# Four reorderings in a one-core encoder step: scaling by the final norm, a deferred pair, the root's argument, a later total

## The chip, the cores and the metric

The kernel runs on one core of a Trainium2 chip. The core has five engines that run side by side and wait for each other by semaphores: TensorE (PE in the profile, with its weight loads as PEld), VectorE (DVE), ScalarE (ACT), GpSimd (POOL) and SyncE (SP). Transfers between device memory and on-chip memory are issued by SP, ACT or POOL. The metric is the time of one execution on the device in microseconds (us); the median of several runs counts.

## The reference

One layer of a streaming encoder on 576 rows (512 of a prompt and 64 of a running stream) with 1024 features, in float32:

```python
x = x + 0.5 * swiglu_ffn(rms_norm(x, ffn1_norm), ffn1_w_gate_up, ffn1_w_down)
h = rms_norm(x, mix_norm); p = h @ w_in
a_b, a_c, a_v, b_u, gate_a, gate_b = jnp.split(p, cuts, axis=-1)
a_conv, new_a = causal_depthwise_conv(a_c * a_v, hist_a, conv_a_w)       # 3 taps
y_a = (a_b * a_conv) @ w_a_out
glu = b_u[..., :D_B] * jax.nn.sigmoid(b_u[..., D_B:])
b_conv, new_b = causal_depthwise_conv(glu, hist_b, conv_b_w)             # 31 taps
y_b = jax.nn.silu(layer_norm(b_conv + conv_b_bias, ...)) @ w_b_out
x = x + (jax.nn.sigmoid(gate_a) * y_a + jax.nn.sigmoid(gate_b) * y_b) @ w_out
x = x + 0.5 * swiglu_ffn(rms_norm(x, ffn2_norm), ffn2_w_gate_up, ffn2_w_down)
y = rms_norm(x, final_norm)                                              # 0.5 is the macaron half step
```

`swiglu_ffn` is `(silu(gate) * up) @ w_down` with 2816 hidden features; `rms_norm` divides by the root of the mean of squares.

## The kernel before

Features lie on the 128 partitions and rows along the free axis: X is eight tiles of 128 x 576 (`X[0]` to `X[7]`). Every product is made in float32 accuracy from three products of rounded parts: a weight and an activation are each split into a high part (`fp32r`) and the low rest, and `mm` issues high x high, high x low and low x high, for two halves of 288 rows. So a product of one output tile over 1024 inputs is 8 x 6 = 48 matmuls, and its result lies in one of four PSUM buffers (tag `mm`, two banks each).

**Weights.** `Stream` keeps them coming. SP loads a raw block (`raw`, six buffers); ACT rounds it into the high part (CAST) and writes its negative into the low part's buffer (ACTIVATE); POOL issues a transfer that adds the raw block to that (`DMA_DIRECT2D u<-raw`, `g<-raw` or `act<-raw`). So a unit's low part is there when that transfer has landed. `get(n)` starts the units up to six ahead. In the two feed-forward stages a hidden tile is made from seven half-sized products instead of eight (`pair`; a scheme after Strassen), for which sums of raw blocks are made on DVE (`w<-raw,raw`, `w<-w,raw`), and whose low parts come from a DVE subtraction (`g<-w,g`, `u<-w,u`).

**Order.** Nothing reorders the instructions: each engine runs them as the code issues them. `product` issues the matmuls of one tile, and what follows them on DVE and ACT is kept back (`behind`) until the next product's matmuls are issued; `rest` is the same for steps of `pair`, of which one is taken up after each of the next pair's seven products.

**Norms.** `Sum` adds up the squares of the eight tiles; `gather` splits the sum and `total` multiplies it by ones on PE, which adds over the partitions. `rstd` makes the reciprocal root of a total: ACT's Abs_reciprocal_sqrt reads the total, DVE's `tensor_scalar` makes the argument `a` from it, and three DVE steps refine the root to `R`. ACT functions sit in tables; a function of another table brings an `ACT_TABLE_LOAD` into ACT's stream. `table(func)` calls a function on one column so that its table is loaded there.

**The stages.** First feed-forward `f1` (from 28 us in the profile), with plain pairs for the first three hidden tiles; `finish1` with the last group's products and the squares of the new X; the mixer with its two convolutions (DVE's taps); LayerNorm in steps that `advance` takes up between the products `("p", 5, j)` and `("ya", j)`: stage 1 subtracts the mean, stage 2 gathers the squares, stage 3 makes the root `RL`; then the second branch, the output projection `("o", j)` in the order `IN_TURN`, and the second feed-forward `f2` with one plain pair (`PLAIN = {"f1": 3, "f2": 1}`). Its last group (`finish2`) makes the tiles 2 to 7 (`LATE`) in two spans of rows (`LATE_SPANS`, 304 and 272 rows), so that the output of the first span leaves while the second is computed; `put` scales the eight tiles by the final norm (ACT), makes the root, multiplies (POOL for the first span, DVE and POOL for the second) and issues the output's transfers.

Of the kernel before, what the change touches and what calls it, by code (L numbers as in the profile page):

```python
# [11 lines left out]
ALU = mybir.AluOpType  # L12
# [91 lines left out]
def tile_encoder_step(  # L104
# [435 lines left out]
    def rstd(total, spans=HALVES):  # L540
# [135 lines left out]
    def ffn(f, xg, sums, finish, forms, R=None, todo=()):  # L676
# [5 lines left out]
        def plain(i, hs):  # L682
# [92 lines left out]
    def finish1(g, hs):  # L775
        ps = both([("f1", "d", g, j) for j in range(2)], hs)
# [199 lines left out]
    stage = [0]  # L976

    def advance():
# [58 lines left out]
    forms = Forms(R_N2)  # L1037
    for n, j in enumerate(IN_TURN):
# [18 lines left out]
    def finish2(g, hs):  # L1057
# [10 lines left out]
        def put(spans, engines, pieces, queues):  # L1068

            i, e = spans[0]  # L1070
            n = e - i
            ys = []
            for q in range(KT // 2):
                yt = gtile(n=2 * n).rearrange("p (a n) -> p a n", a=2)
                for a in range(2):
                    sca.activation(
                        yt[:, a, :], X[2 * q + a][:, i:e], AF.Copy, scale=par(2 * q + a, R_NF)
                    )
                ys.append(yt)
            RF = rstd(fsum, spans)[:, i:e]  # L1080
            for n, (q, a, size) in enumerate(pieces):
                for b in range(a, a + size):
                    engines[q].tensor_tensor(ys[q][:, b, :], ys[q][:, b, :], RF, op=ALU.mult)
                queues[n % 2].dma_start(ydst[q, :, a : a + size, i:e], ys[q][:, a : a + size, :])

        for spans in LATE_SPANS:
            i, e = spans[0]
            fsum.n = LATE[0]
            for j in LATE:
                if i == 0:  # L1090
# [4 lines left out]
                xj = X[j][:, i:e]  # L1095
# [3 lines left out]
                if i > 0 and j == LATE[0]:  # L1099
                    put(  # L1100
# [60 lines left out]
```

## Time and profile before

| | |
|---|---|
| median of 3 runs | 1324.33 us (1319.91, 1324.33, 1324.44) |
| the profiled execution | 1321.72 us, of which 1319.9 from the first to the last instruction (the span) |
| mean granted TensorE clock | 0.994 |
| DVE, ACT, POOL busy | 895.2, 776.6, 400.9 us |
| transfers | 217.22 MB, 165 GB/s in the mean |
| table loads on ACT | 10, of 1.28 us |

Times are from the start of the span. A row of a timeline has the start, the length, the engine, the source line (a helper's line, 80, for nearly all), the operation, out<-in by tile names, the sizes, how many equal instructions are merged, and in brackets the engine's idle time before it with what ended it. A row of windows has the stretch, its length, the busy time (and count) of PE, PEld, DVE, ACT and POOL, then the granted clock, the transfers' share and GB/s.

### The profile page before, as it was taken

The page shows a single profiled execution, that of the slowest core. Times are in us where ns is not written, and L with a number is a line of the kernel's source. Part 1 is how long each engine was busy: PE and PEld are TensorE (multiplying, and loading weights), DVE is VectorE, ACT ScalarE, POOL GpSimd, SP SyncE. Part 2 cuts the span into 40 slices and gives each one's busy share as a digit, 9 for nine tenths or more (in the row PEclk, how much of TensorE's full clock was granted, in tenths as well). Part 3 has the DMA queues.
Part 4 walks back from the last instruction along what each step waited for, and adds up shares of the span by engine and source line. Part 5 has one row for each costly group of instructions (what it writes and reads, how often), then busy time and mean ns, then how long its engine had stood idle before and what let it go on. Part 6 is the DMA issues. An engine that isn't in the chain of part 4 may idle for free.

```text
span 1319.9 us, 25704 instructions
## 1 busy us (share of the span) xinstructions
PE 1292.0 (98%) x9746; PEld 1286.4 (97%) x9746; DVE 895.2 (68%) x1468; ACT 776.6 (59%) x1369; POOL 400.9 (30%) x504
## 2 busy tenths in 40 slices
PE   8999999999999999999999999999899999999995
PEld 8999999999999999999999999999899999999995
DVE  6848758748845999889884061337757858847944
ACT  8655656646766655555545574466665655645663
POOL 4142332332243454322322322221242242231242
PEclk9999999999999999999999999999999999999997
DMA  9497787886798898777875977775687797796692
GB/s 244 103 183 160 157 181 159 173 187 143 154 198 175 172 205 178 168 168 170 173 162 120 201 161 154 167 150 129 133 177 162 154 193 156 158 210 139 152 181 76
DMA packets 289564, 217.22 MB, mean 165 GB/s; under 512 B 15648, under 2 KB 251168, under 8 KB 289440
## 3 DMA queue, kind: packets, MB, share of 16 engines
q0 software_dynamic: 60192, 99.12, 45.7%
q1 hardware_dynamic: 227504, 115.62, 30.8%
q8 instruction: 77, 1.26, 0.4%
q10 hardware_dynamic: 1744, 0.84, 0.2%
q14 instruction: 47, 0.39, 0.1%
HBM read 113.81 MB, written 2.62 MB: 88 GB/s over the span
## 4 chain that ended last, share of the span: by engine, by line
PE 71%; issue 12%; DMA 6%; DVE 4%; ACT 4%; POOL 2%; POOLq 0%; DVEq 0%; SPq 0%; ACTq 0%
PE mm L80 71%; DMA u<-raw 2%; DVE tmp L80 1%; DMA raw<-in_ffn_w_gate_up_dram 1%; DMA raw<-in_ffn_w_down_dram 1%; DMA g<-raw 1%; ACT g L80 1%; ACT tmp L80 1%; ACT act L80 1%; ACT u L80 1%; POOL g L80 1%; DVE acc L80 1%; DVE w L80 1%; DVE g L80 1%; DMA act<-raw 1%
## 5 line engine op out<-in xcount | busy, mean ns | idle before, releaser
L80 PE MATMUL mm<-act,u 128*128 128x288 f32 x4668 | 661.1, 294 | 1.7 <-DMA u<-raw 1.5
L80 PEld LDWEIGHTS mm<-act,u 128*128 128x128 f32 x4668 | 630.9, 188 | 2.4 <-DMA u<-raw 2.1
L80 PE MATMUL mm<-act,g 128*128 128x288 f32 x2748 | 396.4, 294 | 6.1 <-DMA g<-raw 3.8
L80 PEld LDWEIGHTS mm<-act,g 128*128 128x128 f32 x2748 | 374.0, 188 | 7.5 <-DMA g<-raw 4.7
L80 POOL DMA_DIRECT2D u<-raw x203 | 177.0, 872 | 553.1 <-ACT u L80 497.0
L80 PE MATMUL mm<-act,act 128*128 128x288 f32 (+2 forms) x2280 | 314.0, 294 | 2.6 <-DVE act L80 1.6
L80 PEld LDWEIGHTS mm<-act,act 128*128 128x128 f32 x2280 | 303.7, 188 | 4.0 <-DVE act L80 2.3
L80 POOL DMA_DIRECT2D g<-raw x123 | 107.3, 873 | 256.7 <-ACT g L80 202.4
L80 DVE SCALAR_TENSOR_TENSOR w<-g,prm,w 128x606 f32<-128x606 f32 x232 | 179.2, 842 | 1.4 <-ACT w L80 1.4
L80 ACT CAST u<-raw 128x512 fp32r<-128x512 f32 (+2 forms) x203 | 116.4, 574 | 100.6 <-PE mm L80 81.7
L80 DVE TENSOR_TENSOR tmp<-mm,tmp 128x288 f32<-128x288 f32 (+1 forms) x244 | 109.5, 457 | 73.4 <-PE mm L80 56.1
L80 ACT ACTIVATE u<-u 128x512 fp32r<-128x512 f32 (+2 forms) x203 | 120.6, 594 | 6.4
L80 POOL DMA_DIRECT2D act<-raw x92 | 80.9, 879 | 55.5 <-ACT act L80 54.6
L80 ACT CAST g<-raw 128x512 fp32r<-128x512 f32 (+2 forms) x123 | 67.2, 547 | 42.4 <-PE mm L80 15.6
L80 DVE SCALAR_TENSOR_TENSOR tmp<-mm,r 128x576 f32<-128x576 f32 x48 | 36.3, 757 | 78.4 <-PE mm L80 78.4
L80 ACT CAST act<-tmp 128x576 fp32r<-128x576 f32 x84 | 56.3, 674 | 55.6 <-DVE tmp L80 54.7
L80 ACT CAST g<-w 128x512 fp32r<-128x512 f32 x80 | 49.5, 619 | 65.3 <-DVE w L80 59.0
L80 ACT CAST u<-w 128x512 fp32r<-128x512 f32 x80 | 49.5, 619 | 63.3 <-DVE w L80 52.5
L80 DVE TENSOR_TENSOR act<-tmp,act 128x576 fp32r<-128x576 f32 x84 | 62.1, 753 | 19.9 <-ACT act L80 18.6
L80 ACT CAST act<-raw 128x512 fp32r<-128x512 f32 (+2 forms) x101 | 58.7, 582 | 25.1 <-PE mm L80 13.8
L80 ACT ACTIVATE g<-g 128x512 fp32r<-128x512 f32 (+2 forms) x123 | 69.9, 568 | 3.9
L80 DVE TENSOR_TENSOR w<-raw,raw 128x512 f32<-128x512 f32 x80 | 54.8, 685 | 8.6 <-DMA raw<-in_ffn_w_gate_up_dram 8.6
(87 smaller groups left out, 813.5 us busy)
## 6 DMA issues: line engine op xcount, KB each, us to landing
raw<-in_ffn_w_gate_up_dram SPq DMA_DIRECT2D x173, 256.0 KB, 3.5
u<-raw POOLq DMA_DIRECT2D x145, 256.0 KB, 3.9
raw<-in_w_in_dram SPq DMA_DIRECT2D x112, 256.0 KB, 3.3
act<-raw POOLq DMA_DIRECT2D x80, 256.0 KB, 4.6
raw<-in_ffn_w_down_dram SPq DMA_DIRECT2D x96, 192.0 KB, 3.5
g<-raw POOLq DMA_DIRECT2D x65, 256.0 KB, 3.8
g<-raw POOLq DMA_DIRECT2D x42, 192.0 KB, 4.4
u<-raw POOLq DMA_DIRECT2D x42, 192.0 KB, 4.4
```

Source lines behind the costliest of these rows:

```text
L80: return self.tc.keep_in_program_order(fn(*args, **kwargs))
```

## The change

Five edits:

1. `rstd` makes the argument `a` on DVE first, from the total in PSUM; ACT's root then reads `a` from SBUF instead of the total. (All six roots.)
2. `table(AF.Abs_reciprocal_sqrt)` is called at the head of `finish1` and ahead of the output projection, so the table is loaded there instead of right before the root. Ten table loads stay ten.
3. In `f2`, the plain pair's gate, hidden product and split go into `rest`: they are taken up after the first three products of the next pair.
4. `advance` lets one turn pass before stage 3, so LayerNorm's second total and its root come one product later.
5. In `finish2`, a tile's scaling by the final norm (`gained`) follows its square at once, in both spans, instead of all eight in `put`; the multiplication by the root takes two tiles in one instruction (608 or 544 columns), on POOL for the first span and all on DVE for the second (one of four was on POOL before); the second span's six output transfers become four.

```diff
@@ rstd
-        sca.activation(shaped(y), tot, AF.Abs_reciprocal_sqrt, scale=1.0 / D, bias=eps)
         dve.tensor_scalar(shaped(a), tot, 1.0 / D, EPS, op0=ALU.mult, op1=ALU.add)
+        sca.activation(y, a, AF.Abs_reciprocal_sqrt)
@@ ffn, plain
             ups = product(up, xg, got=got)
-            dve.tensor_tensor(halves(t), ps, halves(R), op=ALU.mult)
-            sca.activation(t, t, AF.Silu)
+            hs.append(None)
+            at = len(hs) - 1
+
+            def gate():
+                dve.tensor_tensor(halves(t), ps, halves(R), op=ALU.mult)
+                sca.activation(t, t, AF.Silu)
+
+            def hidden():
+                dve.tensor_tensor(halves(t), ups, halves(t), op=ALU.mult)
+                hs[at] = high(t)
+
+            def parts():
+                hs[at] = hs[at], low(t, hs[at])
+
+            if f == "f2":
+                rest.extend((gate, hidden, parts))
+                return
+            gate()
             forming()
-            dve.tensor_tensor(halves(t), ups, halves(t), op=ALU.mult)
-            hs.append(split(t))
+            hidden()
+            parts()
             forming()
@@ finish1; and ahead of the output projection's loop
+        table(AF.Abs_reciprocal_sqrt)
@@ advance
+        elif stage[0] == 3 and not held[0]:
+            held[0] = 1
+            return
         elif stage[0] == 3:
             RL = rstd(var)
@@ finish2
+        def gained(j, span):
+            n = span.stop - span.start
+            q, a = j // 2, j % 2
+            if a == 0:
+                ys[q] = gtile(n=2 * n).rearrange("p (a n) -> p a n", a=2)
+            sca.activation(ys[q][:, a, :], X[j][:, span], AF.Copy, scale=par(j, R_NF))
...
+            RF = rstd(fsum, spans)[:, i:e].unsqueeze(1).broadcast_to((P, 2, e - i))
             for q in range(KT // 2):
-                yt = gtile(n=2 * n).rearrange("p (a n) -> p a n", a=2)
-                for a in range(2):
-                    sca.activation(
-                        yt[:, a, :], X[2 * q + a][:, i:e], AF.Copy, scale=par(2 * q + a, R_NF)
-                    )
...
+                engine.tensor_tensor(ys[q], ys[q], RF, op=ALU.mult)
+                queues[q % 2].dma_start(ydst[q, :, :, i:e], ys[q])
...
                 fsum.square(X[j], span=span)
                 fsum.add(dve)
+                if j == LATE[0]:
+                    for b in range(LATE[0]):
+                        gained(b, span)
+                gained(j, span)
...
-            spans, (dve, pool, dve, dve),
-            ((0, 0, 1), (0, 1, 1), (1, 0, 2), (2, 0, 2), (3, 0, 1), (3, 1, 1)),
-            (nc.sync, sca),
+        put(spans, dve, (nc.sync, sca))
```

How the order changes at three places. The first is DVE at the start of the second feed-forward, from the last weight sum before the root. (The plain pair is `tmp<-mm,r` for the gate, `tmp<-mm,tmp` of 576 for the hidden product and `act<-tmp,act` for its low part; the rows with w, g, u and raw are weights of the first two pairs; `tmp<-mm,tmp` of 288 is a step of the first pair.) Before:

```order
L80 TENSOR_TENSOR w_11404<-w_11249,raw_11123 128x512
L80 TENSOR_SCALAR tmp_11414<-mm_11417 128x576
L80 SCALAR_TENSOR_TENSOR tmp_11415<-r_11416 128x576
L80 TENSOR_TENSOR tmp_11415<-tmp_11415,tmp_11414 128x576
L80 SCALAR_TENSOR_TENSOR r_11416<-tmp_11415,r_11416 128x576
L80 TENSOR_TENSOR tmp_11341<-mm_11342,r_11416 128x576
L80 TENSOR_TENSOR tmp_11341<-mm_11427,tmp_11341 128x576
L80 TENSOR_TENSOR act_11481<-tmp_11341,act_11479 128x576
L80 TENSOR_TENSOR g_11412<-w_11404,g_11411 128x512
L80 TENSOR_TENSOR w_11488<-raw_11167,raw_11200 128x512
L80 TENSOR_TENSOR w_11514<-w_11488,raw_11346 128x512
L80 TENSOR_TENSOR tmp_11483<-mm_11501,tmp_11483 128x288
```

And after:

```order
L80 TENSOR_TENSOR w_11408<-w_11253,raw_11127 128x512
L80 TENSOR_SCALAR tmp_11418<-mm_11421 128x576
L80 SCALAR_TENSOR_TENSOR tmp_11419<-r_11420 128x576
L80 TENSOR_TENSOR tmp_11419<-tmp_11419,tmp_11418 128x576
L80 SCALAR_TENSOR_TENSOR r_11420<-tmp_11419,r_11420 128x576
L80 TENSOR_TENSOR g_11416<-w_11408,g_11415 128x512
L80 TENSOR_TENSOR w_11485<-raw_11171,raw_11204 128x512
L80 TENSOR_TENSOR tmp_11345<-mm_11346,r_11420 128x576
L80 TENSOR_TENSOR w_11513<-w_11485,raw_11350 128x512
L80 TENSOR_TENSOR tmp_11345<-mm_11431,tmp_11345 128x576
L80 TENSOR_TENSOR tmp_11480<-mm_11498,tmp_11480 128x288
L80 TENSOR_TENSOR act_11553<-tmp_11345,act_11534 128x576
```

The low part of a weight (g) and a sum of raw blocks now stand ahead of the gate, and the plain pair's three steps lie among the next weights.

The second is ACT at the same place, from the cast of the sum above. (`r` is the root, `tmp<-tmp` is Silu, `act<-tmp` the hidden tile's high part, `u` and `g` from raw are weights whose transfer POOL issues next.) Before:

```order
L80 CAST g_11411<-w_11404 128x512
L80 ACT_TABLE_LOAD
L80 ACTIVATE r_11416<-mm_11417,eps 128x576
L80 ACT_TABLE_LOAD
L80 ACTIVATE tmp_11341<-tmp_11341 128x576
L80 CAST act_11479<-tmp_11341 128x576
L80 CAST u_11490<-raw_11038 128x512
L80 ACTIVATE u_11491<-u_11490 128x512
L80 CAST g_11516<-raw_11346 128x512
L80 ACTIVATE g_11517<-g_11516 128x512
```

And after:

```order
L80 CAST g_11415<-w_11408 128x512
L80 ACTIVATE r_11420<-tmp_11418 128x576
L80 CAST u_11487<-raw_11042 128x512
L80 ACTIVATE u_11488<-u_11487 128x512
L80 ACT_TABLE_LOAD
L80 ACTIVATE tmp_11345<-tmp_11345 128x576
L80 CAST g_11515<-raw_11350 128x512
L80 ACTIVATE g_11516<-g_11515 128x512
L80 COPY tmp_11480<-mm_11498 128x288
L80 CAST act_11534<-tmp_11345 128x576
```

One table load is gone from here, the root reads the argument, and the first weight's cast has passed the Silu and the hidden tile's cast.

The third is ACT at the end, the second span's last squares (`tmp<-x`), scalings (`g<-x,gains`) and root. Before:

```order
L80 ACTIVATE tmp_16373<-x_95 128x272
L80 ACTIVATE g_16375<-x_88,gains 128x272
L80 ACTIVATE g_16375<-x_89,gains 128x272
L80 ACTIVATE g_16378<-x_90,gains 128x272
L80 ACTIVATE g_16378<-x_91,gains 128x272
L80 ACTIVATE g_16381<-x_92,gains 128x272
L80 ACTIVATE g_16381<-x_93,gains 128x272
L80 ACTIVATE g_16384<-x_94,gains 128x272
L80 ACTIVATE g_16384<-x_95,gains 128x272
L80 ACTIVATE r_16389<-mm_16390,eps 128x272
```

And after:

```order
L80 ACTIVATE tmp_16310<-x_92 128x272
L80 ACTIVATE g_16313<-x_92,gains 128x272
L80 ACTIVATE tmp_16335<-x_93 128x272
L80 ACTIVATE g_16313<-x_93,gains 128x272
L80 ACTIVATE tmp_16359<-x_94 128x272
L80 ACTIVATE g_16362<-x_94,gains 128x272
L80 ACTIVATE tmp_16384<-x_95 128x272
L80 ACTIVATE g_16362<-x_95,gains 128x272
L80 ACTIVATE r_16389<-tmp_16387 128x272
```

Between the last square (x_95) and the root stands one scaling instead of eight. On PE, the four matmuls of LayerNorm's second total (`mm<-tmp,ones_r`) move behind one more product of 48 matmuls; nothing else moves there.

More of the change, by code (lines that the diff above doesn't have):

```diff
@@ L974, in ya_of @@
         return then
-    stage = [0]
+    stage, held = [0], [0]
     def advance():
@@ L1037, in tile_encoder_step @@
     forms = Forms(R_N2)
+    table(AF.Abs_reciprocal_sqrt)
     for n, j in enumerate(IN_TURN):
@@ L1094, in finish2 @@
                     mm(ps, w, kk, hs[k], k == 0, k == len(hs) - 1, spans)
-                xj = X[j][:, i:e]
+                xj = X[j][:, span]
                 dve.scalar_tensor_tensor(
```

31 lines of the change are left out of this document (10 added, 21 removed).

## The prediction

> **What bounds the kernel now.** I read the page's busy shares first, then the timeline of TensorE (PE) alone for every idle stretch, then a timeline of all engines around the stretches that the change touches.
>
> ```profile
> PE 1292.0 (98%) x9746; PEld 1286.4 (97%) x9746; DVE 895.2 (68%) x1468; ACT 776.6 (59%) x1369; POOL 400.9 (30%) x504
> ```
>
> PE is busy for 1292.0 of 1319.9 us, and the change neither adds nor removes a matmul. It can win or lose only in the 27.9 us in which PE is idle, or by the clock that PE is granted. These are PE's idle stretches that lie near an edit (start and length of the work that follows; in brackets the idle time before it and what ended it):
>
> ```profile
> 30.38 3.40 PE L80 MATMUL mm<-act,g 128*128 128x288 f32 x24 [0.92 <-DVE tmp L80]
> 57.81 1.58 PE L80 MATMUL mm<-act,g 128*128 128x288 f32 x10 [1.70 <-DMA g<-raw]
> 718.32 0.40 PE L80 MATMUL mm<-tmp,ones_r 128*128 128x288 f32 x1 [1.12 <-ACT tmp L80]
> 719.12 0.74 PE L80 MATMUL mm<-tmp,ones_r 128*128 128x288 f32 x3 [0.39 <-DVE tmp L80]
> 933.74 1.59 PE L80 MATMUL mm<-act,g 128*128 128x288 f32 x10 [1.38 <-DVE g L80]
> 937.12 1.60 PE L80 MATMUL mm<-act,u 128*128 128x288 f32 x10 [1.52 <-DMA u<-raw]
> 949.57 1.60 PE L80 MATMUL mm<-act,g 128*128 128x288 f32 x10 [1.03 <-DMA g<-raw]
> 1284.46 7.20 PE L80 MATMUL mm<-act,act 128*128 128x304 f32 x52 [0.95 <-DMA act<-raw]
> ```
>
> Four places matter: LayerNorm's second total (718), the start of the second feed-forward (934 to 950), the first root (30), and what follows PE's last matmul.
>
> **LayerNorm's total.** Its four matmuls wait for operands that ACT and VectorE (DVE) have only just made; the change puts a product of 48 matmuls ahead of them. The rows: a total that did not wait (698) and the product behind it, the product behind this one, and two windows with the granted clock (the third figure from the end); last, where DVE first uses the root.
>
> ```profile
> 697.55 0.69 PE L80 MATMUL mm<-tmp,ones_r 128*128 128x288 f32 x4
> 698.08 3.32 PE L80 MATMUL mm<-act,u 128*128 128x288 f32 x24
> 719.65 4.83 PE L80 MATMUL mm<-act,u 128*128 128x288 f32 x24
> ...
> 716.20:719.60 3.40, 1.89 (x12) 1.44 (x11) 1.52 (x2) 2.54 (x5) 0.00 (x0) 0.99 0.38 110
> 719.60:723.00 3.40, 3.40 (x16) 3.40 (x15) 0.00 (x0) 3.34 (x5) 1.72 (x2) 0.50 0.56 93
> ...
> 760.03 1.42 DVE L80 TENSOR_TENSOR g<-g,r 128x576 f32<-128x576 f32 x2
> ```
>
> The stall is 1.12 us, plus what the total itself took too long: 719.65 - 718.32 = 1.33 instead of 698.08 - 697.55 = 0.53, so 1.92 in all. Right behind it the clock stands at 0.50, and 24 matmuls take 4.83 instead of 3.32: another 1.51. With a product of some 6.5 us (2 x 3.32) in front, the operands (ready by 719.1) are there long before the total. The root comes one product later; DVE uses it at 760, some 30 us after it is ready, so nothing waits. **Gain 3.4** (1.9 if the clock would fall anyway). [...]
>
> **Second feed-forward's start.** The plain pair (product, root, gate, Silu, hidden product, split) stands today on DVE and ACT ahead of the weights of the next pairs; PE waits three times for those weights.
>
> ```profile
> 922.79 0.68 DVE L80 TENSOR_TENSOR w<-w,raw 128x512 f32<-128x512 f32 x1
> 924.21 1.28 ACT L80 ACT_TABLE_LOAD   x1
> 925.50 0.74 ACT L80 ACTIVATE r<-mm,eps 128x576 f32<-128x576 f32 x1
> 926.27 0.76 DVE L80 TENSOR_SCALAR tmp<-mm 128x576 f32<-128x576 f32 x1 [2.80 <-ACT r L80]
> 928.52 0.76 DVE L80 SCALAR_TENSOR_TENSOR r<-tmp,r 128x576 f32<-128x576 f32 x1
> 929.32 0.76 DVE L80 TENSOR_TENSOR tmp<-mm,r 128x576 f32<-128x576 f32 x1
> 930.11 0.69 ACT L80 ACTIVATE tmp<-tmp 128x576 f32<-128x576 f32 x1 [2.57 <-DVE tmp L80]
> 930.36 1.74 PE L80 MATMUL mm<-act,u 128*128 128x288 f32 x12
> 932.20 0.61 ACT L80 CAST u<-raw 128x512 fp32r<-128x512 f32 x1
> 933.00 0.68 DVE L80 TENSOR_TENSOR g<-w,g 128x512 fp32r<-128x512 f32 x1
> 933.77 0.86 POOL L80 DMA_DIRECT2D u<-raw  x1 [9.28 <-ACT u L80]
> 941.58 0.69 ACT L80 ACTIVATE tmp<-tmp 128x576 f32<-128x576 f32 x1 [0.85 <-DVE tmp L80]
> 943.73 0.86 POOL L80 DMA_DIRECT2D g<-raw  x1 [3.68 <-DVE w L80]
> ```
>
> Worked through in the new order: the table is already there and the root's argument goes first, so DVE's TENSOR_SCALAR starts when w is done (923.5) and ends at 924.25, ACT's root runs 924.3 to 925.0, and three DVE steps of 0.78 end at 927.35 (now 929.28). Next on DVE is g<-w,g, done at 928.1 instead of 933.68: the wait at 933.74 goes. On ACT the cast of u<-raw follows the root at 925.0 instead of 932.20; POOL's transfer, 1.57 behind the cast, starts at 926.6 and lands after the same 3.35 at 930: the wait at 937.12 goes (without the idle 1.38 and 1.52, PE would want it at 934.2). The third wait is another matter. Its cast stands on ACT behind the next Silu (941.58), and that behind a run of DVE work that is nearly dense. Counting that run again from 927.35 with the rows' lengths, with the new order's waits for Silu (0.1), for a copy on ACT (0.7) and for a cast (0.1), I get to the Silu at 939.0, 2.6 earlier. The transfer then starts at 941.15; with today's 5.84 to landing (943.73 to 949.57) PE goes on at 947.0, a gain of 2.6; with the 3.35 of the one at 933.77 it would land at 944.5, ahead of PE, which without any of the three waits would be there at 945.6 (949.57 - 3.93), and all 3.9 are gained. **Gain 3.1**, nearer the lower end, since the transfers around this one move along with it (2.6 to 3.9).
>
> A buffer of PSUM is let go by the gate (929.32) and taken by PE's fifth product of the pair (930.36), which PE comes to no earlier than now. The gate now stands behind two weight steps on DVE, but by the sum above it ends at 929.4, so it is not late.
>
> **The root's argument first.** Today ACT reads the total, and DVE's TENSOR_SCALAR waits until it has; afterwards DVE reads it and ACT waits for DVE. Both are chains of the same two steps, so the turn itself is worth nothing where no table load overlaps. At the first root one does:
>
> ```profile
> 28.80 0.72 ACT L80 ACTIVATE r<-mm,eps 128x576 f32<-128x576 f32 x1
> 29.56 0.76 DVE L80 TENSOR_SCALAR tmp<-mm 128x576 f32<-128x576 f32 x1 [3.42 <-ACT r L80]
> ```
>
> TENSOR_SCALAR can run while the table loads, so the PSUM buffer for which PE waits 0.92 at 30.38 is free in time, and R comes 0.6 earlier. PE then meets the next wait at 57.81, which ends 0.6 earlier because the run of DVE and ACT work before it starts from R. **Gain 0.6** (0 to 0.65); the idle stretch there grows from 1.70 to 2.0.
>
> **Table loads moved.** Ten stay ten. The two new early ones (1.28 plus 0.2 each) stand on ACT ahead of casts for weights six units ahead. The rows are the slack that ACT has there at the first feed-forward's end, and in the late phase where the eight scalings by final norm are now slipped in:
>
> ```profile
> 374.36 0.51 ACT L80 CAST g<-raw 128x384 fp32r<-128x384 f32 x1 [1.33 <-PE mm L80]
> ...
> 1278.92 0.51 ACT L80 CAST act<-raw 128x384 fp32r<-128x384 f32 x1 [1.91 <-DMA raw<-in_ffn_w_down_dram]
> ```
>
> The first takes up 1.33 of 1.48, and PE has no wait before 718, so 0. The three scalings (3 x 0.45) fit into the 1.91, so the wait at 1284.46 stays as it is. If those covers are gone, each costs at most what it lasts, 1.5.
>
> **After the last matmul.** Each tile's scaling by final norm now follows its square; before, all eight stood between the last square and the root.
>
> ```profile
> 1297.18 0.44 DVE L80 TENSOR_TENSOR acc<-acc,tmp 128x272 f32<-128x272 f32 x1
> 1298.53 0.90 DVE L80 TENSOR_TENSOR acc<-acc,tmp 128x272 f32<-128x272 f32 x1 [0.56 <-ACT tmp L80]
> ...
> 1305.51 3.39 ACT L80 ACTIVATE g<-x,gains 128x272 f32<-128x272 f32 x8
> 1305.66 0.72 PE L80 MATMUL mm<-tmp,ones 128*128 128x272 f32 x2
> 1308.81 0.46 ACT L80 ACTIVATE r<-mm,eps 128x272 f32<-128x272 f32 x1
> 1309.31 0.44 DVE L80 TENSOR_SCALAR tmp<-mm 128x272 f32<-128x272 f32 x1 [4.16 <-ACT r L80]
> 1311.08 3.32 DVE L80 TENSOR_TENSOR g<-g,r 128x272 f32<-128x272 f32 x6
> ```
>
> PE's total ends at 1306.38. TENSOR_SCALAR then ends at 1306.9, ACT's root at 1307.4, and DVE's three steps at 1308.8 instead of 1311.05. Four multiplications of 544 (0.72 each, between the 0.68 of 512 and the 0.76 of 576 above) end at 1311.5; six of 272 ended at 1314.4. That is 2.9 earlier, but 1.1 MB (four tiles of 128 x 544 x 4 bytes) now leaves within 2 us instead of 3, so I take 0.4 off: **gain 2.5** (2 to 3).
>
> **Sum.** 3.4 + 3.1 + 0.6 + 2.5 = 9.6 us. The profiled execution took 1321.72 (span 1319.9), which gives 1312.1. The median of the runs is 1324.33, 2.6 above it; I forecast 1313.5 for the median.
>
> **Rivals.** (1) The third wait does not move: its transfer lands at 949.57 whatever comes before. The second feed-forward then gains 0 and the sum is 6.5, 1315.2 against the profiled time. Against it: that transfer starts 0.3 us after ACT's cast, which does move.
> (2) The clock falls at another place. The stall at 718 left PE busy for 1.89 of 3.40 us; the one at 937 left as little and kept its clock:
>
> ```profile
> 934.40:937.80 3.40, 1.88 (x15) 1.64 (x14) 3.13 (x6) 2.39 (x6) 1.09 (x2) 1.00 0.82 138
> ```
>
> So we are at the edge, and 2.0 idle at 57 may fall over it: 1.5 less, a sum of 8.1, 1313.6.
> (3) Slower: the clock falls at 57 and stays at 0.50. It costs 1.51 in 3.4 us, 0.44 per us, so from 22 us on the gain is eaten, and from 37 us (9.6 + 6.6 = 16.2 lost) the kernel is slower by over 0.5%: 1328.3. Against it: at 719.6 it lasted one window.
> (4) POOL in the way of DVE: DVE's addition takes 0.44 alone and 0.90 beside POOL's multiplications, which are now twice as long. If an addition always waits for a whole one of them (1.7), the last tile's update comes up to 0.7 later: a sum of 8.9, 1312.8. [...]
> (5) The turned root does nothing at 30: 9.0, 1312.7.
>
> **How the numbers follow.** Forecast with (4) and (5), which change little: 0.68; (1) 0.15; (2) 0.14; (3) 0.03. A change of 0.5% (6.6 us) is about what this measurement can tell from none. (1) lies on that bound, so most of it and some of the forecast, where two terms come out at their lower ends, count as no change: faster 0.75, the same 0.22, slower 0.03. The range goes from 1308 (every term at its upper end, 11.0, off the lowest run, 1319.91, and one more, since that run need not be the lowest there is) to 1320.4 (LayerNorm's 1.9 and the tail's 2.0 alone, off the median).
>
> **What would show it.** No PE wait at LayerNorm's total and no window at 0.50 there; at the second feed-forward one wait of up to 1.5 us left, for a DMA; from PE's last matmul to the end about 11 us instead of 13.5. Wrong if PE waits for DVE in the first two pairs of the second feed-forward, if a new wait at 1284 is over 1.5, or if a window at 0.50 turns up elsewhere.

## The result and the profile after

The changed kernel takes 1304.77 us (median of five executions: 1304.43 to 1305.48, and one of 1310.95) where the kernel before took 1324.33 in the same timing (1319.68 to 1327.78). The ratio is 0.987, 95% interval 0.9836 to 0.9904. The forecast was 1313.5 with a range of 1308.0 to 1320.4: the direction was right, the gain between the medians was 19.6 us where 10.8 was forecast, and the median lies 3 us below the range.

The profile after is of the execution of 1310.95 us (span 1309.2), not of a typical one. Its busy shares:

```profile
PE 1292.7 (99%) x9746; PEld 1288.2 (98%) x9746; DVE 894.7 (68%) x1466; ACT 775.9 (59%) x1371; POOL 398.2 (30%) x498
```

TensorE's stretches that begin with a wait near an edit, in the same view as before the change:

```profile
56.30 1.59 PE L80 MATMUL mm<-act,g 128*128 128x288 f32 x10 [1.07 <-DMA g<-raw]
365.53 3.76 PE L80 MATMUL mm<-act,u 128*128 128x288 f32 x26 [0.41 <-DMA u<-raw]
944.66 1.59 PE L80 MATMUL mm<-act,g 128*128 128x288 f32 x10 [0.49 <-DMA g<-raw]
1279.45 7.19 PE L80 MATMUL mm<-act,act 128*128 128x304 f32 x52 [0.91 <-DMA act<-raw]
1299.48 0.72 PE L80 MATMUL mm<-tmp,ones 128*128 128x272 f32 x2 [0.54 <-ACT tmp L80]
```

The waits at 30 and 718 are gone, and of the three near 934 to 950 only 0.49 of the third is left. There is a new one of 0.41 at 365 us. LayerNorm's second total now lies among the products without a gap, and no window there is at 0.50:

```profile
723.08 3.29 PE L80 MATMUL mm<-act,act 128*128 128x288 f32 x24
726.21 0.69 PE L80 MATMUL mm<-tmp,ones_r 128*128 128x288 f32 x4
726.74 3.32 PE L80 MATMUL mm<-act,u 128*128 128x288 f32 x24
```

The end, from TensorE's last total (its row is above, it ends at 1300.20):

```profile
1300.24 0.44 DVE L80 TENSOR_SCALAR tmp<-mm 128x272 f32<-128x272 f32 x1 [1.28 <-PE mm L80]
1300.72 0.43 ACT L80 ACTIVATE r<-tmp 128x272 f32<-128x272 f32 x1 [0.88 <-DVE tmp L80]
...
1302.61 2.63 DVE L80 TENSOR_TENSOR g<-g,r 128x544 f32<-128x544 f32 x4
```

DVE is done at 1305.24 and the span ends at 1309.2: 9.0 us behind the last matmul, where it was 13.5.

Profile against profile it is 10.8 less (1321.72 to 1310.95), against a sum of 9.6. That these come near is chance: from 412 to 690 us, where no edit acts, the profile after falls 3.6 us behind the one before (the same matmul is 0.5 earlier at 412 and 3.1 later at 690). What needs an explanation is that the four other executions are 6 us quicker than the profiled one. No idle time of TensorE can hold that. The cause shows where the prediction did not look, in how many matmuls go into a stretch in which TensorE is busy all the time. The view of windows, TensorE alone: stretch, length, busy time with the count of matmuls, granted clock. Before:

```profile
420.00:690.00 270.00, 270.00 (x2079) 1.00 0.83 175
725.00:905.00 180.00, 180.00 (x1370) 1.00 0.80 166
```

After, the profiled 1310.95 us:

```profile
420.00:690.00 270.00, 270.00 (x2053) 1.00 0.81 173
725.00:905.00 180.00, 180.00 (x1369) 1.00 0.80 170
```

Same busy time, same clock of 1.00, same shape of matmul, but 26 fewer of them in 270 us: 2053 instead of 2079. The mean distance from one matmul's start to the next, called the step here, is 130.0 ns in the one case and 131.66 ns in the other, for hundreds of us without a change. (Single distances lie between 125 and 134 ns, in a pattern that repeats every 6 matmuls in the first case and every 12 in the second.) In the profile before, the step was 130.0 from 410 to 697 and 131.66 from there to the mixer's end; in the one after, 134.4 from 366 to 409, 131.66 from 410 to 701, 130.0 to 726 and 131.66 from there on. The 3650 mixer matmuls at 1.66 ns are 6.1 us. That was the theory for the first experiments.

### The profile page after: what moved, and what is told of

Its sections match the earlier page's. It is cut to its first block, busy times and chain, and to the rows that moved or that the text cites. A ratio compares the mean times of both kernels' runs of the same rounds, so it can differ in the third digit from the quotient of the medians.

```text
span 1309.2 us, 25706 instructions
## 1 busy us (share of the span) xinstructions
PE 1292.7 (99%) x9746; PEld 1288.2 (98%) x9746; DVE 894.7 (68%) x1466; ACT 775.9 (59%) x1371; POOL 398.2 (30%) x498
## 4 chain that ended last, share of the span: by engine, by line
PE 71%; issue 16%; DMA 6%; POOL 2%; ACT 2%; DVE 1%; POOLq 0%; DVEq 0%; SPq 0%; ACTq 0%
PE mm L80 71%; DMA raw<-in_ffn_w_down_dram 2%; DMA u<-raw 2%; DMA raw<-in_ffn_w_gate_up_dram 1%; POOL g L80 1%; POOL u L80 1%; DMA g<-raw 1%; ACT u L80 1%; DVE tmp L80 1%; DMA act<-raw 1%; ACT g L80 0%; POOL act L80 0%; ACT act L80 0%; ACT tmp L80 0%; DVE g L80 0%
```

## The experiments

In the short diffs, - is the changed kernel unless the kernel before is named. The runs were timed in four batches of four, in the order of their numbers, and the changed kernel itself ran only in the first and the third. The kernel before had medians between 1321.3 and 1324.0 in the four, so a difference of some 2 us against a group of another batch rests on the traces more than on the times.

**The changed kernel again (no edit), twice.**

> The changed kernel once more. Theory (TensorE's own step from matmul to matmul is not fixed: in the profiled 1310.95 us the 128x288 matmuls of the mixer, 410 to 890 us, mostly follow each other in 131.66 ns, in a part of the profile before in 130.0 ns; about 3650 matmuls times 1.66 ns are 6.1 us): a profiled execution near 1304.8 shows 130.0 ns over most of 410 to 890, one near 1311 shows 131.66 again; times fall into clusters, 1304 to 1306 and about 1311. Rival A (the 6 us lie in waits of TensorE that differ from run to run): an execution near 1304.8 has the same step as the one of 1310.95 and some 6 us less idle time of TensorE, which is not possible with the 12 us that the trace has in all unless half of them go. Rival B (granted clock): the difference shows as windows below 1.00; the clocks listed, 0.998 for the slow one and 0.997 for the others, speak against it.

> The changed kernel a third time, for a trace of its quick group. Theory: an execution near 1305 has 130.0 ns from 410 to 694 and from 722 to 910 us, and 131.66 between; one near 1310.5 the reverse. Rival: an execution near 1305 with 131.66 over most of 410 to 910, or the reverse.

The first gave 1305.0, 1305.74, 1306.05, 1310.23, 1310.39 and 1310.8, the second 1303.63 to 1305.68 and one of 1310.94. Over the three timings 12 of 17 executions lie between 1303.6 and 1306.1 (median 1304.8) and five between 1310.2 and 1311.0, none between. The granted clock of both groups is 0.996 to 0.998, so these are two groups at the same clock. The first profile (1310.23) has the step of the slow one shown above, 2052 and 1370 matmuls; the second (1305.68) has the quick step in both stretches:

```profile
420.00:690.00 270.00, 270.00 (x2079) 1.00 0.83 175
725.00:905.00 180.00, 180.00 (x1387) 1.00 0.81 172
```

26 and 18 matmuls more than the profile of 1310.95, at 0.13 us each 5.7 us in these 450 us; the medians of the groups, 1304.8 and 1310.8, are 6.0 apart. The kernel before has 2079 and 1370: quick up to LayerNorm, slow behind it.

**LayerNorm's total put back.**

```diff
-        elif stage[0] == 3 and not held[0]:
-            held[0] = 1
-            return
```

> The changed kernel with LayerNorm's second total put back right behind its gather (no turn passed). The prediction's term: 3.4 us slower than the changed kernel (1308.2), made of a stall of 1.92 and of 1.51 in which the clock stands at 0.50. Theory of the step: 3.4 plus 1.66 ns for each of the some 1300 matmuls from 719 to 890, 2.2 us, if the stall throws TensorE from a step of 130.0 to one of 131.66 ns as in the profile before: 5.6 us, 1310.4. Rival (the clock falls anyway, or the stall is made up later): 1.9 us or less, 1306.7.

Measured 1309.27 to 1311.07 and one of 1315.33, median 1310.6: 5.5 above the changed kernel's quick group (median of the first five, 1310.3, less 1304.8). The profile (1311.07) has the waits of 1.12 and 0.40 again, and the step goes from 130.0 to 131.66 at 697 and stays there to 905 (2079 and 1369 matmuls). Set against the quick run with the mixer's total twice (below), the same matmul starts 2.2 us later behind the stall and another 2.2 later at 910. The clock did not fall here:

```profile
716.20:719.60 3.40, 1.88 (x12) 1.45 (x11) 1.91 (x3) 2.72 (x5) 0.64 (x1) 1.00 0.27 77
719.60:723.00 3.40, 3.40 (x28) 3.40 (x27) 0.78 (x2) 3.34 (x6) 1.09 (x2) 1.00 0.81 139
```

28 matmuls in the second window where the profile before had 16 at 0.50. So the size (3.4) was near, but made of other things: 2.2 of stall, 2.2 of step, and the half clock only in some executions. The rest of the 5.5 is not at LayerNorm: this profile also waits 0.18 and 0.68 at 1272 and 1275 for weights of the late phase, which the quick profile (1305.68) does not.

**The plain pair at once again.**

```diff
-            if f == "f2":
-                rest.extend((gate, hidden, parts))
-                return
```

> The changed kernel with the second feed-forward's plain pair worked off at once again (gate, Silu, hidden product and split ahead of the next pair's weights; the root's argument stays first and the table stays loaded). The prediction's term of 3.1 us is for the whole start of the second feed-forward, of which the root that comes some 2 us earlier stays here. Expected by the traces: 2 to 4 us slower than the changed kernel, 1307 to 1309, with TensorE waiting for g<-w,g and for u<-raw again near 925 to 940. Rival (the earlier root alone does it): under 0.7 us, 1304.8 to 1305.5.

1307.54, 1307.87, 1307.97, 1309.18, 1309.25 and 1316.33: 2.7 to 4.4 above the middle of the quick group. In the profile (1309.18) two of the old waits are back, 1.53 at 928 and 1.93 at 941, and behind the second a window of 3.4 us stands at 0.50.

**The scalings last again** (the old last group: eight scalings in `put`, six multiplications, one tile of four on POOL, six transfers).

> The changed kernel with the last group of the second feed-forward as before: all eight scalings by the final norm between the last square and the root, six multiplications of 272 columns and six transfers. The prediction's term: 2.5 us slower than the changed kernel (2 to 3), 1307.3. The two traces, from TensorE's last matmul to the end, 13.5 us before and 9.0 after: 4.5 us slower, 1309.3. Here the root's argument comes first, so that the old order may lose up to 0.5 less.

1310.32 to 1311.67 and 1315.01 to 1315.92, three each; median 1313.34. Group against group that is 6.5 (1311.32 less 1304.8) and 4.2 (1315.04 less 1310.8). Profile against profile, both of the slow group (1315.01 here, 1310.23 of the changed kernel), it is 4.8, none of it ahead of the late phase. (The quick group here was not profiled, so its 6.5 is not accounted for.) The end comes 13.1 us behind the last matmul instead of 9.0, and TensorE waits 0.93 ahead of the total.

**The root as before** (ACT reads the total; the two early `table` calls taken out).

```diff
+        sca.activation(shaped(y), tot, AF.Abs_reciprocal_sqrt, scale=1.0 / D, bias=eps)
         dve.tensor_scalar(shaped(a), tot, 1.0 / D, EPS, op0=ALU.mult, op1=ALU.add)
-        sca.activation(y, a, AF.Abs_reciprocal_sqrt)
```

> The changed kernel with the root as before (ACT reads the total first, DVE's TENSOR_SCALAR behind it) and without the two early table loads. The prediction's term for the first root is 0.6 us; the second feed-forward's root loses its early table too, about 1.5 us there, of which waits for weights may show up to 1.5. Quick executions (the changed kernel has two groups, around 1305 and around 1310.5): 1305.5 to 1307. Rival (the turned root carries more of the gain than was priced): 1308 or more. Beside that: without finish1's table load TensorE should have no wait near 366 us; if that wait made the group, the executions fall into one group only; if not, into two as before.

1306.02 to 1306.83 and 1312.19 to 1312.98, three each: 1.8 and 1.9 above the groups. The wait at 30 is back (1.01), and 1.0 of waits at 924 and 939. TensorE still waits 0.26 at 366 without finish1's table load, and both groups are there: that load makes neither the wait nor the groups.

**POOL at the end, in the changed kernel and taken out of the one before.** The closing instructions by their line hold the 2 us by which the end was quicker than forecast. The kernel before, then the changed one (form: shortest, median and longest in ns, first and last start):

```profile
L1151 POOLq DRAIN  x3: 34/102/7913, 1311.2 to 1319.6; - x3
L1151 SPq DRAIN  x3: 7/7/7, 1317.1 to 1319.4; - x3
```

```profile
L1170 POOLq DRAIN  x3: 34/93/12543, 1290.0 to 1308.9; - x3
L1170 SPq DRAIN  x3: 7/7/7, 1308.3 to 1308.6; - x3
```

Before, SP has seen the last transfer land by 1317.1; POOL's DRAIN, begun at 1311.2, lasts 7.91 us to 1319.13, and all engines are let go behind it. After, POOL's long DRAIN ends at 1302.5, ahead of the transfers. In both it ends 6.09 us behind POOL's last multiplication (1313.05 and 1296.41). SP's waits in the profile before show the same 2 us, though under the name of PE's sequencer, whose part in the closing had long been done:

```profile
SPq L1151 <- PEq L1151: 2.7, 2, 2.2
```

The first test puts one of the four last multiplications on POOL:

```diff
-                engine.tensor_tensor(ys[q], ys[q], RF, op=ALU.mult)
+                (pool if q == 1 else engine).tensor_tensor(ys[q], ys[q], RF, op=ALU.mult)
```

> The changed kernel with one of the last four multiplications of 544 columns on POOL instead of DVE. Theory (POOL's closing DRAIN ends 6.1 us after POOL's last multiplication, and the end waits for it: 1313.05 to 1319.13 in the profile before, 1296.41 to 1302.53 in the one after): the multiplication ends about 1.8 us behind DVE's root, the DRAIN 6.1 later, the span another 0.75 later: from TensorE's last matmul to the end 11 us instead of 9.0, the kernel 2 us slower than the changed one (quick executions at 1307). Rival (the end waits for the output's transfers only): DVE is done 0.6 us earlier, 8.5 to 9.2 us from the last matmul to the end, no slower.

The second takes POOL's share out of the kernel before:

```diff
-            spans, (dve, pool, dve, dve),
+            spans, (dve, dve, dve, dve),
```

> The kernel before with POOL's two last multiplications of 272 columns given to DVE (eight on DVE, none on POOL), nothing else. Theory (POOL's closing DRAIN, 6.1 us behind its last work, sets the end): DVE ends up to 0.7 us later, the transfers land near 0.5 later (1317.5 instead of 1317.0 in the profile), the end follows 0.8 behind that: 12.0 us from TensorE's last matmul to the end instead of 13.5, 1.5 us faster than the kernel before. Rival (the transfers set it): 0 to 0.7 us slower.

With POOL the changed kernel's quick executions take 1305.8 to 1307.27, its others 1312.45 and 1313.06: 2 slower in each group (1306.6 and 1312.8 in the middle). Its profile:

```profile
1296.86 1.77 POOL L80 TENSOR_TENSOR g<-g,r 128x544 f32<-128x544 f32 x1 [6.33 <-DVE r L80]
```

```profile
L1170 POOLq DRAIN  x3: 34/93/7890, 1296.8 to 1305.2; - x3
L1170 SPq DRAIN  x3: 7/7/7, 1302.8 to 1305.0; - x3
```

POOL ends at 1298.63, the DRAIN at 1304.72, again 6.09 later, while the transfers are down at 1302.8. From the last matmul to the end it is 11.17 us instead of 8.96. In the kernel before without POOL it is 11.02 instead of 13.52: DVE ends 0.4 earlier although it does two multiplications more, and the other 2.1 are the DRAIN. (12.0 was expected, with DVE ending later; but its eight multiplications took 2.91, where six had taken 3.32 beside POOL's.) Its whole time (1317.84 to 1325.53, median 1321.53; ratio 0.9995, 0.9978 to 1.0012) can't show 2.5 us, since the kernel before spreads over 8 to 12 us in its timings. The theory holds by the traces.

**Can the step be turned by the totals?** In all traces so far the mixer's step changes only at totals: near 410, 697 and 722.

```diff
-            RL = rstd(var)
+            RL = rstd(var, times=2)        # total: the four matmuls issued twice
```

(The lines that hand `times` on to the loop in `total` are left out.)

> The changed kernel with the four matmuls of LayerNorm's second total issued twice (the same values into the same buffer, 0.5 us more). Theory (each total turns TensorE's step from 130.0 to 131.66 ns or back: at 410, 697 and 722 us in the traces): doubled, it turns it twice and so not at all; an execution that had 130.0 from 410 to 694 then has 131.66 from 694 to 910, one that had 131.66 has it to 701 and 130.0 from there to 910. The two groups, 1305 and 1310.5, move together: 1307.9 and 1308.8. Rival (the groups come from something before or behind the mixer): they stay 5.5 us apart, 1305.5 and 1311.

The same for the mixer's first total, twice and three times (`R = rstd(ss, times=2)`, `times=3`):

> The changed kernel with the four matmuls of the mixer's first total (near 410 us, the root of the mixer's norm) issued twice, 0.5 us more. Theory (the time is set by how many of the mixer's matmuls step at 131.66 instead of 130.0 ns, and the total near 410 decides which): the profiled execution lies within 1 us of 1305.7 + 1.66 ns times its matmuls at 131.66 between 410 and 910 us beyond the 215 of the stretch 694 to 722; the shares of the two groups may shift, their distance stays 5 to 6 us unless one of them is gone. Rival (the groups come from something else in the execution): the profile's step and its time do not go together.

> As the run with the total twice, but three times (1.0 us more than the changed kernel). Theory: the profiled execution within 1 us of 1306.2 + 1.66 ns times its matmuls at 131.66 between 410 and 910 us beyond 215; if the total only turns the step, three turns are as one, and the groups are those of the changed kernel, 1306 and 1311.5. Rival: as there.

The first expectation failed: 1304.01, 1304.62, 1304.94 and 1311.6, 1311.72, 1311.87, the groups further apart than before. In its profile (1311.87) the doubled total turned 130.0 into 131.66 as a single one does. So a total may change the step, but two do not cancel, and my rule is wrong. The other two have groups as before (1304.09 to 1304.92 and 1310.21 to 1311.75; 1305.44, 1306.47 and 1309.62 to 1312.17), and in both the time goes with the step: the profile of 1304.92 has 2079 and 1387 matmuls, the one of 1312.17 has 2053 and 1370 (within 1 us of the formula in both). In every profile of a kernel with the two groups, nine of nine by then, the upper group has the slow step and the lower the quick one.

**Another order of the six matmuls.** This one acts on the step itself.

```diff
-SIX = ((0, 0), (1, 0), (0, 1), (1, 1), (2, 0), (2, 1))
+SIX = ((0, 0), (0, 1), (1, 0), (1, 1), (2, 0), (2, 1))
```

> The changed kernel with another order of the six matmuls that stand for one float32 matmul pair: both halves of each part together (high x high, high x high, high x low, high x low, low x high, low x high) instead of two parts of one half in turn. Theory (the step is a pattern over these six, and settles into one of several): a step of another length, one value or several between 126 and 136 ns, so that the time moves by up to 4 ns times 4900 matmuls, 20 us, either way, and the two groups 5.5 us apart are gone or at another distance. Rival (the groups have nothing to do with the six): 1305 and 1310.5 again.

All twelve executions lie in 1317.32 to 1320.28, median 1317.89; the groups 5.5 us apart are gone. The mixer has one step in the whole profile, 133.33 ns, at the same clock:

```profile
420.00:690.00 270.00, 270.00 (x2027) 1.00 0.81 170
725.00:905.00 180.00, 180.00 (x1352) 1.00 0.79 166
```

From 410 to 910 us there are some 3800 matmuls at 130.0; 3.33 ns more for each is 12.7 us, and 1304.8 + 12.7 = 1317.5. Two more orders, `((0, 0), (1, 0), (2, 0), (0, 1), (1, 1), (2, 1))` and `((0, 0), (1, 0), (0, 1), (1, 1), (2, 1), (2, 0))`:

> The changed kernel with the three parts of the first half and then those of the second (high x high, high x low, low x high; and again). Theory (the step belongs to the order of the six): a step of its own, between 126 and 136 ns, and its own group or groups; time 1305 plus 4900 matmuls times its difference from 130.0 ns, within 3 us. Rival: 1305 and 1310.5 again.

> The changed kernel with only the last two of the six turned (low x high of the second half before that of the first). Same theory: a step of its own, time 1305 plus 4900 matmuls times its difference from 130.0 ns, within 3 us. Rival: 1305 and 1310.5 again, since the same two halves and weights follow each other in four of six places.

Both have 133.33 ns in the mixer as well, and one group: 1319.91 to 1322.62 (median 1320.93) and 1319.57 to 1321.83 (1320.63). They are 3 us above the first other order, because the second feed-forward's products step differently too: from 960 to 1270 us it is 131.6 ns in the mean of the first one's profile and 132.7 in theirs, 2.6 us for 2340 matmuls. The expectation, 1305 + 4900 x 3.33 ns = 1321.3, was met within 0.7 us in number, but by the profiles only 12.3 of its 16.3 us lie in the mixer. The original order is the quickest of the four, in either of its groups.

**The change without the two steps.** With the first other order, LayerNorm's total put back, and the kernel before:

> The order of parts of the earlier run (1317.9, one group, step 133.33 ns) and LayerNorm's second total put back right behind its gather. Theory (with the changed kernel's own order the edit was worth 5.3 us, of which about 2 are the step that the stall leaves at 131.66): where there is only one step, the edit is worth the prediction's 3.4 us (stall 1.92, half clock 1.51): 1321.1 to 1321.5. Rival A (the step is not part of it): 5.3 again, 1323. Rival B (the clock falls only with the other order): 1.9, 1319.8.

> The kernel before with the same other order of parts. Against the changed kernel with it (1317.9) this is the whole change without the step's two values. The prediction's sum: 9.6, 1327.5. The sum of the terms as the runs have them, without the step: LayerNorm 3.4, second feed-forward 2.8, root 1.4, tail 4.6 to 5.5, 12.2 to 13.1: 1330 to 1331. Theory of the groups: one group here too (spread under 3 us), where the kernel before had 1317.4 to 1328.1. Rival (the spread of the kernel before comes from elsewhere): a spread of 8 to 10 us.

LayerNorm: 1318.72 to 1322.81, median 1320.75, 2.9 more than 1317.89. In its profile the stall costs 1.8 us (starts of the same matmul ahead of and behind it) and the clock stays at 1.00; the profiled execution also has the longer step in the second feed-forward, so that 1.8 to 2.9 is all that can be said. It is not 5.3: the step was part of that. The 1.51 of half clock that was expected here did not come.

The kernel before: 1330.33 to 1332.79, median 1331.53. One group with a spread of 2.5 where the same kernel in its own order has 1316.37 to 1328.18. So most of that spread belongs to the order of the six as well. The whole change is worth 13.6 us here by the medians (12.2 to 13.1 was expected), where the mixer's step does not move. The two profiles lie 15.5 apart, of which 12.3 are counted by idle time: 0.9 at the start, 1.8 at LayerNorm, 4.2 of waits near 943 to 960 (1.23, 1.53 and 1.47, none after), 0.8 ahead of the last total, 4.6 behind it. The other 3.2 are mostly the second feed-forward's step, 131.6 ns in the changed kernel's profile and 132.7 in this one, so that the 13.6 may hold some of that too.

## Why the prediction was too cautious

The same matmul's start in the profile before (1321.72) and in the quick one after (1305.68) gives the account, 16.0 in all:

| place | forecast | measured |
|---|---|---|
| start, up to 90 us (the root's argument first) | 0.6 | 0.7 |
| LayerNorm's total | 3.4 | 3.7 |
| TensorE's step, 725 to 905 us | not in the sum | 2.2 |
| second feed-forward's start | 3.1 | 4.0 |
| late phase and end | 2.5 | 5.4 |

**The step that failed first** is the one that opens the argument: "It can win or lose only in the 27.9 us in which PE is idle, or by the clock that PE is granted." TensorE's own rate at full clock was not a constant. In the profile before, the total at 697 turned the step from 130.0 to 131.66 ns, and the stalled total at 718 left it there for the mixer's remaining 1370 matmuls (725 to 905 us). In the quick profile after, the later total, which does not stall, turned it back to 130.0 at 722. So the edit gave 2.2 us in which TensorE had been busy. Shown by: the put-back total (2.2 us at the stall and 2.2 more by 910), and the other order of the six, with which the step stays and the edit is worth at most 2.9. Whether the stall or the place of the total decides this was not separated.

**The end** was sized at 2.5 and measured 5.4. What was priced came out as priced. DVE was to end 5.1 us behind the last matmul and ended 5.03 behind it, 3.0 earlier than before. (The sum has a slip of 0.2: four multiplications of 0.72 from 1308.8 end at 1311.7, not 1311.5; but the four took 2.63.) SP sees the last transfer land 3.1 behind DVE's end (1305.24 to 1308.3) instead of 2.7 (1314.4 to 1317.1), which is the 0.4 that was taken off. The failing step is that the sum ends there: with "so I take 0.4 off: **gain 2.5**" it takes DVE and the transfers for all that holds the end, and puts POOL's DRAIN at nothing. Before the change the DRAIN set the end, 2.0 us behind the transfers; after it, the DRAIN is done ahead of them. Its row was there to be read in the profile before; I had priced the move of POOL's share to DVE as DVE time alone. Shown by both POOL runs. The other 0.8 is the wait ahead of the last total (1.34 before, 0.54 after), which the sum did not have:

```profile
1304.85 0.72 PE L80 MATMUL mm<-acc,ones 128*128 128x272 f32 x2 [1.34 <-DVE acc L80]
```

**Second feed-forward's start.** The mechanism was right and the lower end was taken: "Gain 3.1, nearer the lower end" should have been the upper, 3.9. The Silu ahead of the third weight came at 937.9, where 939.0 was counted, and POOL's issue at 940.05 instead of 941.15:

```profile
937.90 0.69 ACT L80 ACTIVATE tmp<-tmp 128x576 f32<-128x576 f32 x1 [0.85 <-DVE tmp L80]
940.05 0.86 POOL L80 DMA_DIRECT2D g<-raw  x1 [3.69 <-DVE w L80]
```

TensorE went on at 944.66, 4.6 us behind the issue, between the two prices given (5.84 and 3.35). It waited 0.49 here, 0.68 in another profile of the changed kernel and not at all in the third. Rival 1 did not come. The two edits share this place: the root and its table alone are 1.1 to 2.1 of it (starts of the same matmul in the run with the root as before, against the three profiles of the changed kernel), the deferral 2.7 to 4.4 by its run; together they gave 4.0, near the lower end of their sum.

**LayerNorm.** The size was right, the parts were not all of them lasting. The fall to 0.50 took part in the profile before, and not behind the same stall in the runs with the total put back, with POOL taken out of the kernel before, or in the two with the other order. Rival 2 (the fall happens elsewhere) was real: in the quick profile after, it fell at 58 us,

```profile
57.19 2.15 PE L80 MATMUL mm<-act,g 128*128 128x288 f32 x10 [1.82 <-DMA g<-raw]
```

```profile
57.96:61.37 3.41, 3.41 (x17) 3.41 (x16) 3.13 (x6) 2.40 (x6) 1.03 (x2) 0.50 0.96 192
```

(17 matmuls where a full window has 28: 1.4 us), while in the profiled 1310.95 the wait there was 1.07 and the clock held. The same stall keeps the clock in one execution and loses it in another for one window of 3.41 us: at LayerNorm's total, waits of 1.12 and 0.39 stand ahead of 0.50 in the profile before, waits of 1.12 and 0.40 ahead of 1.00 with the total put back; at 57 us the wait of 1.82 above was enough, and one of 1.73 without POOL in the kernel before was not.

The times of the clock's changes also tell apart an execution that lost the clock at this stall and one that kept it. In the profiles before and after, each change comes a whole number of 3.413 us behind the first entry of the clock in the trace (at 6.18 us before, at 3.85 after): the fall at 719.57 is 209 times 3.413 later, the return at 722.98 210 times, and the fall behind the last matmul 381 times in both (1306.66 and 1304.33). In the profile before, the stall at 718 lies whole in one such window, the last before the fall. Without POOL in the kernel before, the edge at 718.43 cuts the same stall in two:

```profile
716.15:719.57 3.42, 1.91 (x12) 1.00 0.39 114
...
715.01:718.43 3.42, 2.30 (x17) 1.00 0.60 162
718.43:721.84 3.41, 3.01 (x23) 1.00 0.28 48
```

The windows ahead of the three falls hold 11 (the pair at once, 942.82), 12 (before, 719.57) and 13 matmuls (the quick profile after, 57.96), where a full one holds 28. The two that share the stall without POOL hold 17 and 23 and keep the clock, and one of 13 keeps it too (56.24 to 59.65 without POOL). So the 1.51 came at this total where the whole stall lay in one window and not where an edge cut it, and the edges differ between executions; that the edge decides is an inference from these two profiles. The sum had taken the 1.51 as sure. Rival 2's "left as little" compares busy time (1.88 and 1.89); counted from edge to edge, the window at 937 (934.61 to 938.02) holds 14 matmuls and the one at 718 holds 12.

**The root and the tables.** 0.6 at the start came out at 0.7, in part by luck: set against the profile before, the quick one is 1.2 ahead at 40 us and 0.6 at 57, has lost it all by 70 to the half clock, and is 0.7 ahead again at 90, because the waits of 0.55 at 61 and 0.50 at 76 do not come. "The idle stretch there grows from 1.70 to 2.0" did not show as a rule (1.07, 1.33 and 1.82 in the three profiles of the changed kernel). The table load in finish1, priced at 0, stands at 368.5 in the profile after, behind the wait of 0.41 at 365.5, and cannot have made it; the kernel before without POOL waits 0.29 at the same place.

**POOL in DVE's way** (rival 4) happened as described: one addition took 1.68 us beside POOL's multiplication of 608 columns, the next 0.44 alone.

```profile
1295.03 1.68 DVE L80 TENSOR_TENSOR acc<-acc,tmp 128x272 f32<-128x272 f32 x1 [0.50 <-ACT tmp L80]
...
1297.62 0.44 DVE L80 TENSOR_TENSOR acc<-acc,tmp 128x272 f32<-128x272 f32 x1 [0.56 <-ACT tmp L80]
1298.53 0.44 DVE L80 SCALAR_TENSOR_TENSOR x<-mm,x 128x272 f32<-128x272 f32 x1 [0.47 <-PE mm L80]
```

The last tile's update then waited 0.47 for TensorE's product, so DVE had caught up and the end paid nothing for it.

**The forecast for the median.** The sum was set against a profile of the kernel before, and 1.4 was added for the median. With a kernel that runs in two groups, one profile says which group it caught and not how often it comes. The profile before had the quick step up to LayerNorm, the one after the slow step; both medians were of other executions. That draw, which no step of the sum covers, moved the result by 2.3 us: the median after is 0.9 below the quick profile, where I had put it 1.4 above the sum.

Open: what chooses the group. The step is already decided when the mixer begins (131.66 from 366 to 409 in the quick profiles, 130.0 or 134.4 in the slow ones), the waits at 366 (none to 0.41) do not sort them, and what a total does to the step follows no rule that I found. So no version could be built that always falls into the quick group; none of the kernels run here beats the changed kernel.

## What to carry to other kernels

Where one engine is busy 98% of the time, count its instructions in equal stretches of several profiles before taking its rate as fixed: 1% there was 6 us. Time a kernel often enough to see whether it has groups, and compare group with group; a change of 5 us hides or shows by the draw of one profile. Ahead of the end of a kernel, look at the closing instructions of every engine: work that is given to a spare engine at the end may cost more after it than it saves (with one of the last multiplications on POOL, 11.17 us from the last matmul to the end instead of 8.96).

## What the runs showed of the hardware

- TensorE's step between matmuls of 128 x 288, each with its own weights, at a granted clock of 1.00: 130.0 (before the change, 412 to 694 us), 131.66 (before, 726 to 905 us), 133.33 (the other orders of the six) or 134.4 ns (after, 366 to 409 us) in the mean; in the mixer constant over up to 290 us and changed only at a total. Which of them occur depends on the order in which two halves and three parts follow each other (130.0 and 131.66 with one order, 133.33 alone with three others).
- POOL's closing DRAIN ended 6.09 us behind POOL's last multiplication in the profiles before (1313.05 to 1319.13), after (1296.41 to 1302.50) and with POOL at the end (1298.63 to 1304.72), and 6.1 behind it with the scalings last (1306.35 to 1312.4) and without POOL in the last multiplications of the kernel before (1303.09 to 1309.2); the kernel ended behind it in each of the five.
- The granted clock fell to 0.50 for one window of 3.41 us behind stalls of 1.5 to 1.9 us in three profiles (1.12 and 0.39 at 718 before, 1.82 at 57 in the quick one after, 1.93 at 941 with the pair at once), and not behind nearly equal ones in others (1.12 and 0.40 at 718 with the total put back, 1.70 at 57 before). Its changes in the profiles before and after lie on a grid of 3.413 us that starts at 6.18 us in the one and at 3.85 in the other. At LayerNorm's total the clock fell in the profile before, where the whole stall lay in one window of 12 matmuls, and not without POOL, where an edge left 17 and 23 on its sides.
